# Three of seven half-products of an fp32r feed-forward layer read both parts of their operand in one 512-column pass

## The chip, the cores and the metric

One NeuronCore of one Trainium2 chip runs the whole layer. The metric is device time in microseconds (us) of one execution. Before the change three runs took 820.55, 821.32 and 821.43 us, a median of 821.32 us.

## What is computed

One layer of an encoder on 512 tokens of width 1024, in float32: a half-step SwiGLU feed-forward network (FFN1), a mixer (a Fourier part and attention), a second half-step feed-forward network (FFN2), and a last RMS norm.

```python
def swiglu(h, w_gate, w_up, w_down):
    return (jax.nn.silu(h @ w_gate) * (h @ w_up)) @ w_down

x = x + 0.5 * swiglu(rms_norm(x, ffn1_norm), ffn1_w_gate, ffn1_w_up, ffn1_w_down)
...
x = x + 0.5 * swiglu(rms_norm(x, ffn2_norm), ffn2_w_gate, ffn2_w_up, ffn2_w_down)
```

The hidden width is 2752: 21 blocks of 128 columns and one of 64.

## The kernel before

**Precision.** TensorE multiplies in fp32r, which keeps fewer bits than float32. So each operand is split into a high part (a cast to fp32r) and a low part (the rest), and each product is three matmuls: high weights by high operand, high weights by low operand, low weights by high operand. The high part is cast by ScalarE, the low part subtracted by VectorE (`lows`, L128). Another way to a low part is `rest_by_dma` (L155): ScalarE writes the negated high part, and a DMA from GpSimd's queue adds the weights to it as they come from memory.

**Half-products.** A block j of 128 hidden columns needs a gate product and an up product, each of 128 weights columns by 512 tokens, over 8 chunks of 128 rows. For 35 blocks of the two networks (17 in FFN1, 18 in FFN2) `seven` (L407) makes these two products from seven products of half the tokens (256 columns) and half the rows (4 chunks), with sums and differences of weights' quarters and of the operand's quarters. The weights' names are a11, a12, s1, s2, s4, s3, a22, in order of use; the operand's are b11, b22, b21, t1 to t4, and stand in one tile `rt` with their high and low parts, made once per network in `operands` (L333). `multiply` (L413) makes one half-product: 4 chunks x 3 passes = 12 matmuls of 256 columns, each with a weight load of its own (LDWEIGHTS, "PEld" in the profile). So a block takes 84 matmuls.

**Where the sums are made.** PSUM bank r collects a11, s2, s3 and a22 one after another; ScalarE copies its state out in between (`kept`, L426, and L456, L464). Bank q collects s1 and then s4; bank p2 holds a12. VectorE adds the pieces into the gate `g` (L441, L451) and the up half `u` (L457), multiplies them (L465), and the result is split into `at` (L466, L467). All of these use the first 256 of a bank's 512 columns.

**Order.** PE and SP run in the order of the code, the other engines in an order that the scheduler chose when the kernel was built; each engine takes its instructions strictly in its own order. In `seven`, a block's products run as a11, a12, then a22 of the block before, then s1, s2, s4, s3. Between them `prepare` (L366) makes the next block's weights in eight pieces: raw weights arrive by DMA, VectorE makes the combinations (`combine`, L394), ScalarE casts and VectorE subtracts: three pieces of 1024 columns (`both`, L379: a11 with a12, s1 with s2, s3 with s4) and one of 512 (`single`, L388: a22). a22's weights are needed a whole block later than they are made.

**Stages.** Blocks come in groups. After each group of blocks its down products run (`dn`, L184: 128 weight columns by 512 tokens, three matmuls of 512 columns per chunk). The 512-column passes use `turned` (L177): operand and bank are walked in pieces of 4 columns with a step of 16, four times. Where the 512-column passes read their operand, it starts 4 columns past a multiple of 16 (`NEAR`, `FRONT + LOWER`), and the weights at a multiple of 16; `rt` and its weights both start at a multiple of 16. At the start of each group the second matmul is cut into one of 64 and one of 192 columns (`CUT`, `parts_of`, L160).

## Time and profile before

| | |
|---|---|
| median of three runs | 821.32 us |
| the profiled execution's own time | 820.94 us |
| its span in the profile | 818.9 us |
| PE busy (matmul) | 812.4 us, 99% of the span |
| VectorE busy | 637.5 us, 78% |
| ScalarE busy | 483.1 us, 59% |
| GpSimd busy | 29.3 us, 4% |
| matmuls of the half-products | r 1686, q 840, p 420 pieces |

The profiled execution took 2.0 us more than its span (what lies ahead of the first and behind the last recorded instruction). A row of the groups reads: source line, engine, operation, output tile <- input tiles, shape, count | busy time in us, mean duration of one in ns | idle time before it and what ended that. A matmul's duration is its latency; matmuls are pipelined, so the time from one to the next is shorter, and is read from the chain of work (start, length in us, what, count), where each piece begins as the one ahead of it ends.

### The profile page before, as it was taken

The page shows a single profiled execution, that of the slowest core. Times are in us where ns is not written, and L with a number is a line of the kernel's source. Part 1 is how long each engine was busy: PE and PEld are TensorE (multiplying, and loading weights), DVE is VectorE, ACT ScalarE, POOL GpSimd, SP SyncE. Part 2 cuts the span into 40 slices and gives each one's busy share as a digit, 9 for nine tenths or more (in the row PEclk, how much of TensorE's full clock was granted, in tenths as well). Part 3 has the DMA queues.
Part 4 walks back from the last instruction along what each step waited for, and adds up shares of the span by engine and source line. Part 5 has one row for each costly group of instructions (what it writes and reads, how often), then busy time and mean ns, then how long its engine had stood idle before and what let it go on. Part 6 is the DMA issues. An engine that isn't in the chain of part 4 may idle for free.

```text
span 818.9 us, 13611 instructions
## 1 busy us (share of the span) xinstructions
PE 812.4 (99%) x5362; PEld 746.1 (91%) x5362; DVE 637.5 (78%) x1003; ACT 483.1 (59%) x810; POOL 29.3 (4%) x31
## 2 busy tenths in 40 slices
PE   9999999999999999999999999999999999999997
PEld 7889999899989998889998888899989999899987
DVE  7898896479856847799998578999945896479574
ACT  7763674257523735699998448456632673257462
POOL 0110000000000000221000001100000000000001
PEclk9999999999999999999999999999999999999999
DMA  7664322333141223342101234542232322322222
GB/s 258 174 145 179 124 93 77 124 104 142 59 151 71 90 70 116 129 147 66 65 26 52 77 112 127 123 176 108 94 122 114 127 100 69 132 104 97 69 78 103
DMA packets 31568, 89.97 MB, mean 110 GB/s; under 512 B 3728, under 2 KB 9232, under 8 KB 31504
## 3 DMA queue, kind: packets, MB, share of 16 engines
q1 hardware_dynamic: 27776, 82.61, 29.1%
q0 software_dynamic: 3008, 5.51, 3.7%
q10 hardware_dynamic: 720, 0.98, 0.3%
q8 instruction: 42, 0.69, 0.3%
q14 instruction: 22, 0.18, 0.1%
HBM read 84.24 MB, written 2.10 MB: 105 GB/s over the span
## 4 chain that ended last, share of the span: by engine, by line
PE 95%; DVE 2%; ACT 1%; POOL 1%; issue 1%; DMA 0%; POOLq 0%; DVEq 0%; ACTq 0%
PE dn L184 25%; PE r L420 23%; PE q L420 12%; PE gu L184 8%; PE mix L184 6%; PE p L420 6%; PE gu L709 3%; PE mix L1203 2%; PE mix L1169 2%; PE mix L1007 1%; PE mix L1008 1%; PE mix L1009 1%; PE mix L1066 1%; PE mix L1143 1%; PE mix L1144 1%
## 5 line engine op out<-in xcount | busy, mean ns | idle before, releaser
L420 PE MATMUL r<-rt,ring 128*128 128x256 f32 x1686 | 209.2, 276 | 0.0
L184 PE MATMUL dn<-at,ring 128*128 128x512 f32 x900 | 202.5, 380 | 0.0
L420 PEld LDWEIGHTS r<-rt,ring 128*128 128x128 f32 x1686 | 200.3, 188 | 0.8
L184 PEld LDWEIGHTS dn<-at,ring 128*128 128x128 f32 x900 | 168.0, 188 | 28.3
L420 PE MATMUL q<-rt,ring 128*128 128x256 f32 x840 | 106.6, 276 | 0.0
L128 DVE TENSOR_TENSOR ring<-s,ring 128x1024 fp32r<-128x1024 f32 x70 | 85.5, 1221 | 23.8 <-ACT ring L379 20.8
L420 PEld LDWEIGHTS q<-rt,ring 128*128 128x128 f32 x840 | 100.4, 188 | 0.0
L544 DVE SCALAR_TENSOR_TENSOR gx<-dn,gx 128x512 f32<-128x512 f32 x61 | 41.9, 688 | 67.1 <-PE dn L184 67.1
L379 ACT CAST ring<-s 128x1024 fp32r<-128x1024 f32 x70 | 73.5, 1050 | 28.3 <-PE p L420 13.7
L170 ACT CAST ring<-raw_dn 128x768 fp32r<-128x768 f32 (+3 forms) x58 | 45.3, 784 | 72.8 <-PE dn L184 61.9
L128 DVE TENSOR_TENSOR ring<-raw_dn,ring 128x768 fp32r<-128x768 f32 (+3 forms) x58 | 51.5, 892 | 5.7 <-PE r L420 4.4
L420 PE MATMUL p<-rt,ring 128*128 128x256 f32 x420 | 53.3, 276 | 0.0
L128 DVE TENSOR_TENSOR ring<-raw_g,ring 128x1024 fp32r<-128x1024 f32 x35 | 42.7, 1220 | 11.7 <-PE p L420 10.2
L420 PEld LDWEIGHTS p<-rt,ring 128*128 128x128 f32 x420 | 50.2, 188 | 0.0
L184 PE MATMUL gu<-ring 128*128 128x512 f32 x216 | 48.9, 381 | 0.0
L379 ACT CAST ring<-raw_g 128x1024 fp32r<-128x1024 f32 x35 | 36.8, 1051 | 17.2 <-DMA raw_g<-in_wgu 11.5
L184 PEld LDWEIGHTS gu<-ring 128*128 128x128 f32 x216 | 40.4, 188 | 6.9
L428 ACT COPY p<-r 128x256 f32<-128x256 f32 x35 | 12.9, 369 | 44.9 <-PE r L420 44.6
L452 ACT ACTIVATE g<-g 128x512 f32<-128x512 f32 x35 | 22.2, 633 | 23.9 <-DVE g L451 23.6
L388 ACT CAST ring<-raw_u 128x512 fp32r<-128x512 f32 x35 | 21.8, 624 | 16.0 <-PE q L420 15.7
L184 PE MATMUL mix<-near,ring 128*128 128x512 f32 x120 | 28.8, 381 | 0.0
L465 DVE TENSOR_TENSOR u<-g,u 128x512 f32<-128x512 f32 x35 | 24.0, 687 | 6.1 <-ACT u L464 6.0
(266 smaller groups left out, 1314.3 us busy)
## 6 DMA issues: line engine op xcount, KB each, us to landing
raw_g<-in_wgu SPq DMA_DIRECT2D x35, 512.0 KB, 3.8
raw_u<-in_wgu SPq DMA_DIRECT2D x35, 512.0 KB, 4.3
raw_dn<-in_wd SPq DMA_DIRECT2D x40, 384.0 KB, 3.1
raw_gu<-in_wgu SPq DMA_DIRECT2D x12, 512.0 KB, 3.7
raw_o<-in_wo SPq DMA_DIRECT2D x8, 512.0 KB, 3.5
raw_dn<-in_wd SPq DMA_DIRECT2D x8, 448.0 KB, 3.7
raw_wq<-in_wins SPq DMA_DIRECT2D x4, 512.0 KB, 3.5
raw_f<-in_winf SPq DMA_DIRECT2D x4, 512.0 KB, 3.5
```

Of the source, the lines that this page charges most:

```text
L128: nc.vector.tensor_tensor(out=lo, in0=src, in1=asf(hi), op=ALU.subtract)
L170: nc.scalar.copy(hi[:, :n, :], raw[:, :n, :])
L184: nc.tensor.matmul(ps, a, b, start=first and b is mhi and a is whi, stop=last and a is wlo)
L379: nc.scalar.copy(hi, src)
L388: nc.scalar.copy(hi, src)
L420: nc.tensor.matmul(ps[:, t], a[:, ks], b[:, i, t], start=first and i == 0 and o == 0, stop=i == KH - 1 and o == 2, skip_group_check=not first,
L452: nc.scalar.activation(b["g"], b["g"], AF.Silu)
L465: nc.vector.tensor_tensor(out=u, in0=b["g"], in1=u, op=ALU.mult)
L544: nc.vector.scalar_tensor_tensor(out=x[d][:, t], in0=ps[:, t], scalar=0.5, in1=x[d][:, t], op0=ALU.mult, op1=ALU.add)
L709: nc.tensor.matmul(turned(pss[c]), w[:, k % 2, c], turned(m[k]), start=k == 0 and m is hh and w is hi, stop=k == KD - 1 and w is lo,)
L1169: nc.tensor.transpose(pts[n][:, c * P : (c + 1) * P], prob[t, b, c][:, kc * P : (kc + 1) * P], ident)
L1203: nc.tensor.matmul(turned(outs[t, b]), w, turned(p), start=kc == 0 and i == 0, stop=kc == 3 and i == 1)
```

## The change

Three of the seven, a12, s4 and a22 (`WIDE`), take high weights by both operand parts in one pass: `rt` is laid out so that the high and the low part of a chunk lie side by side (512 columns), and one turned matmul of 512 columns writes high by high into the first half of the bank and high by low into its second half. The low weights by the high part stay a matmul of 256 columns. So these products take 4 x (one of 512 + one of 256) in place of 12 x one of 256. The other four keep their 12 matmuls; only their operand's place changes. What the second half of the bank then holds has to be added: one more VectorE addition of 256 columns for each of the three (`added`, `kept`). And the low part of a22's weights is made by `rest_by_dma` in place of VectorE's subtraction.

```diff
+WIDE = ('a12', 's4', 'a22')
-            rt = ap.tile([P, 7, 2, KH, HALF], F32R, name=f"rt{n_}")
+            rt = ap.tile([P, 7, KH, 2, HALF], F32R, name=f"rt{n_}")
...
-                        h, l = rt[:, c, 0, i], rt[:, c, 1, i]
+                        h, l = rt[:, c, i, 0], rt[:, c, i, 1]
...
                 def single(n, src):
                     t = take()
                     hi, lo = t[:, :S], t[:, S:]
                     nc.scalar.copy(hi, src)
-                    lows(lo, src, hi)
+                    rest_by_dma(lo.rearrange("p (a b) -> p a b", b=P), hi.rearrange("p (a b) -> p a b", b=P), wgu[2 * j + 1][:, KH:])
...
                 def multiply(ps, wn, on, w, first):
-                    (whi, wlo), (mhi, mlo) = w[wn], (part[on][:, i] for i in range(2))
+                    whi, wlo = w[wn]
                     for i in range(KH):
-                        ks = slice(i * P, (i + 1) * P)
-                        for o, (a, b) in enumerate(((whi, mhi), (whi, mlo), (wlo, mhi))):
-                            for t in parts_of(next(count)):
-                                nc.tensor.matmul(
-                                    ps[:, t], a[:, ks], b[:, i, t], start=first and i == 0 and o == 0,
-                                    stop=i == KH - 1 and o == 2, skip_group_check=not first,
-                                )
+                        ks, m = slice(i * P, (i + 1) * P), part[on][:, i].rearrange("p a b -> p (a b)")
+                        start, stop = first and i == 0, i == KH - 1
+                        if wn in WIDE:
+                            nc.tensor.matmul(turned(ps), whi[:, ks], turned(m), start=start, stop=False, skip_group_check=True)
+                        else:
+                            for o in range(2):
+                                for t in parts_of(next(count)):
+                                    nc.tensor.matmul(
+                                        ps[:, t], whi[:, ks], m[:, o * HALF :][:, t], start=start and o == 0, stop=False,
+                                        skip_group_check=True,
+                                    )
+                        nc.tensor.matmul(
+                            ps[:, :HALF], wlo[:, ks], m[:, :HALF], start=False, stop=stop, skip_group_check=True
+                        )
                     give(*w.get((wn, "slots"), ()))

-                def kept(ps, n, j):
-                    t = sp.tile([P, HALF], F32, tag=n, name=f"{n}{n_}_{j}")
-                    nc.scalar.copy(t, ps)
-                    return t
+                def added(out, ps, other, n):
+                    nc.vector.tensor_tensor(out=out, in0=ps[:, :HALF], in1=other, op=ALU.add)
+                    if n in WIDE:
+                        nc.vector.tensor_tensor(out=out, in0=ps[:, HALF:], in1=out, op=ALU.add)
+
+                def kept(out, ps, wide=False):
+                    nc.scalar.copy(out, ps[:, HALF:] if wide else ps[:, :HALF])
+                    if wide:
+                        nc.vector.tensor_tensor(out=out, in0=ps[:, :HALF], in1=out, op=ALU.add)
...
-                        nc.vector.tensor_tensor(out=b["g"][:, HALF:], in0=ps, in1=b["p1"], op=ALU.add)
+                        added(b["g"][:, HALF:], ps, b["p1"], "a12")
...
-                        nc.vector.tensor_tensor(out=b["g"][:, :HALF], in0=b["q"], in1=b["u2"], op=ALU.add)
+                        added(b["g"][:, :HALF], b["q"], b["u2"], "s4")
...
-                        nc.scalar.copy(u[:, HALF:], b["r"])
+                        kept(u[:, HALF:], b["r"], "a22" in WIDE)
```

On PE, at the first products of block 12 of FFN1 (r, p2 and q are the banks, with the block's number behind the first underscore; the last number is a buffer's), there stood before:

```order
L420 MATMUL r0_12_1866<-rt0_129,ring_61 128x256 x12
L420 MATMUL p20_12_1881<-rt0_129,ring_61 128x256 x12
L420 MATMUL r0_11_1744<-rt0_129,ring_61 128x256 x12
L420 MATMUL q0_12_1918<-rt0_129,ring_61 128x256 x12
L420 MATMUL r0_12_1866<-rt0_129,ring_61 128x256 x12
```

Where a11 ends and a12 begins, there stands now:

```order
L425 MATMUL r0_12_1806<-rt0_129,ring_61 128x256 x2
L429 MATMUL r0_12_1806<-rt0_129,ring_61 128x256
L421 MATMUL p20_12_1821<-rt0_129,ring_61 128x4x32x4
L429 MATMUL p20_12_1821<-rt0_129,ring_61 128x256
L421 MATMUL p20_12_1821<-rt0_129,ring_61 128x4x32x4
```

No product moved; in a12, a22 and s4 matmuls of 512 columns (128x4x32x4) and of 256 now alternate, four of each.

On DVE (VectorE), from the gate's sum of block 12 on, there stood before:

```order
L441 TENSOR_TENSOR g0_12_1894<-p20_12_1881,p10_12_1879 128x256
L128 TENSOR_TENSOR ring_61<-raw_g0_13_1860,ring_61 128x1024
L465 TENSOR_TENSOR u0_11_1855<-g0_11_1772,u0_11_1855 128x512
L128 TENSOR_TENSOR ring_61<-s12_0_13_1864,ring_61 128x1024
L128 TENSOR_TENSOR ring_61<-raw_u0_13_1861,ring_61 128x512
L128 TENSOR_TENSOR at0_128<-u0_11_1855,at0_128 128x512
L394 TENSOR_TENSOR s12_0_14_1986<-raw_u0_14_1983 128x512
L451 TENSOR_TENSOR g0_12_1894<-q0_12_1918,u20_12_1945 128x256
L128 TENSOR_TENSOR ring_61<-s34_0_13_1865,ring_61 128x1024
```

There stands now:

```order
L435 TENSOR_TENSOR g0_12_1830<-p20_12_1821,p10_12_1807 128x256
L129 TENSOR_TENSOR ring_61<-raw_g0_13_1800,ring_61 128x1024
L437 TENSOR_TENSOR g0_12_1830<-p20_12_1821,g0_12_1830 128x256
L442 TENSOR_TENSOR u0_11_1795<-r0_11_1692,u0_11_1795 128x256
L129 TENSOR_TENSOR ring_61<-s12_0_13_1804,ring_61 128x1024
L486 TENSOR_TENSOR u0_11_1795<-g0_11_1716,u0_11_1795 128x512
L395 TENSOR_TENSOR s12_0_14_1918<-raw_u0_14_1915 128x512
L435 TENSOR_TENSOR g0_12_1830<-q0_12_1852,u20_12_1879 128x256
L395 TENSOR_TENSOR s12_0_14_1918<-s12_0_14_1918,raw_g0_14_1914 128x512
L437 TENSOR_TENSOR g0_12_1830<-q0_12_1852,g0_12_1830 128x256
L129 TENSOR_TENSOR at0_128<-u0_11_1795,at0_128 128x512
L129 TENSOR_TENSOR ring_61<-s34_0_13_1805,ring_61 128x1024
```

The three additions (L437 twice, L442) are new, the low part of a22's weights (`ring<-raw_u`) is gone, and the low part of s3 and s4 (`ring<-s34`) stands a few rows later.

On ACT (ScalarE), around the copies of bank q (p5) and of bank r (u2) in block 12, there stood before:

```order
L388 CAST ring_61<-raw_u0_13_1861 128x512
L428 COPY p50_12_1931<-q0_12_1918 128x256
L466 CAST at0_128<-u0_11_1855 128x512
L428 COPY u20_12_1945<-r0_12_1866 128x256
L379 CAST ring_61<-s34_0_13_1865 128x1024
```

There stands now:

```order
L389 CAST ring_61<-raw_u0_13_1801 128x512
L440 COPY p50_12_1853<-q0_12_1852 128x256
L158 ACTIVATE ring_61<-ring_61 128x512
L440 COPY u20_12_1879<-r0_12_1806 128x256
L380 CAST ring_61<-s34_0_13_1805 128x1024
L487 CAST at0_128<-u0_11_1795 128x512
```

The negated copy (L158) has come ahead of the copy of r, and the cast of `at` has gone behind the cast of s34.

More of the change, by code (lines that the diff above doesn't have):

```diff
@@ L431, in step, with part_tile @@
+                def kept(out, ps, wide=False):
+                    nc.scalar.copy(out, ps[:, HALF:] if wide else ps[:, :HALF])
+                    if wide:
+                        nc.vector.tensor_tensor(out=out, in0=ps[:, :HALF], in1=out, op=ALU.add)
+                def part_tile(n, j):
+                    return sp.tile([P, HALF], F32, tag=n, name=f"{n}{n_}_{j}")
                 def step(j, w, n):
@@ L433, in step @@
                     if n == 0:
-                        b["r"] = bank(f"r{n_}_{j}")[:, :HALF]
+                        b["r"], b["p1"] = bank(f"r{n_}_{j}"), part_tile("p1", j)
                         multiply(b["r"], "a11", "b11", w, True)
-                        b["p1"] = kept(b["r"], "p1", j)
+                        kept(b["p1"], b["r"])
                     elif n == 1:
-                        ps = bank(f"p2{n_}_{j}")[:, :HALF]
+                        ps = bank(f"p2{n_}_{j}")
                         multiply(ps, "a12", "b21", w, True)
                         b["g"] = tp.tile([P, S], F32, tag="g", name=f"g{n_}_{j}")
-                        nc.vector.tensor_tensor(out=b["g"][:, HALF:], in0=ps, in1=b["p1"], op=ALU.add)
+                        added(b["g"][:, HALF:], ps, b["p1"], "a12")
                     elif n == 3:
-                        b["q"] = bank(f"q{n_}_{j}")[:, :HALF]
+                        b["q"], b["p5"] = bank(f"q{n_}_{j}"), part_tile("p5", j)
                         multiply(b["q"], "s1", "t1", w, True)
-                        b["p5"] = kept(b["q"], "p5", j)
+                        kept(b["p5"], b["q"])
                     elif n == 4:
                         multiply(b["r"], "s2", "t2", w, False)
-                        b["u2"] = kept(b["r"], "u2", j)
+                        b["u2"] = part_tile("u2", j)
+                        kept(b["u2"], b["r"])
                     elif n == 5:
                         multiply(b["q"], "s4", "b22", w, False)
-                        nc.vector.tensor_tensor(out=b["g"][:, :HALF], in0=b["q"], in1=b["u2"], op=ALU.add)
+                        added(b["g"][:, :HALF], b["q"], b["u2"], "s4")
                         nc.scalar.activation(b["g"], b["g"], AF.Silu)
@@ L455, in step @@
                         b["u"] = tp.tile([P, S], F32, tag="u", name=f"u{n_}_{j}")
-                        nc.scalar.copy(b["u"][:, :HALF], b["r"])
-                        nc.vector.tensor_tensor(
-                            out=b["u"][:, :HALF], in0=b["u"][:, :HALF], in1=b["p5"], op=ALU.add
-                        )
+                        u = b["u"][:, :HALF]
+                        if "s3" in WIDE:
+                            nc.scalar.copy(b["u"], b["r"])
+                            nc.vector.tensor_tensor(out=u, in0=u, in1=b["u"][:, HALF:], op=ALU.add)
+                            nc.vector.tensor_tensor(out=u, in0=u, in1=b["p5"], op=ALU.add)
+                        else:
+                            nc.scalar.copy(u, b["r"][:, :HALF])
+                            nc.vector.tensor_tensor(out=u, in0=u, in1=b["p5"], op=ALU.add)
                     elif n == 9:
```

## The prediction, made before the result was known

> **What bounds the kernel now.** I read the page first, for the engines' shares, then who waited for whom, then the chain of work, for the pace. Two lines of the page:
>
> ```profile
> span 818.9 us, 13611 instructions
> PE 812.4 (99%) x5362; PEld 746.1 (91%) x5362; DVE 637.5 (78%) x1003; ACT 483.1 (59%) x810; POOL 29.3 (4%) x31
> ```
>
> and all rows in which PE waited for anything:
>
> ```profile
> PE busy L654 <- PEq L1519: 0.8, 1, 0.8
> PE mix L1143 <- DVE near L128: 0.2, 1, 0.2
> ```
>
> TensorE is never waited into idleness in the half-products. Its busy share alone would not say that it is at its pace, but the two waits of 1.0 us in all do. So the time is the sum of the start-to-start times of the matmuls, and the chain gives these:
>
> ```profile
> 75.65 1.36 PE p L420 x12
> 130.05 3.96 PE dn L184 x18
> 134.01 1.37 PE r L420 x12
> 135.38 27.72 PE dn L184 x126
> ```
>
> In a long run a pass of 256 columns takes 1.36 us / 12 = 113.3 ns and one of 512 columns 3.96 us / 18 = 220.0 ns. From 256 to 512 columns 106.7 ns are added, so a pass has 113.3 - 106.7 = 6.7 ns on top of its columns. That is all that the change can save on TensorE.
>
> The skill says otherwise about this size: the Trainium skill, "TensorE: Matmul & The Clock Gate", section "Back-to-back issue gap", puts the fixed part of a pass at 2.5 ns. By that the joined passes would save 420 x 2.5 = 1.05 us in place of the 2.8 us below. The rows above measure 6.7 ns in this kernel's fp32r stream, and the measurement decides.
>
> **Part 1, the joined passes.** 35 blocks x 3 products x 4 chunks = 420 times, three passes of 256 (340.0 ns) become one of 512 and one of 256: 220.0 + 113.3 = 333.3 ns. If both kept the pace of their long runs, that would be 420 x 6.7 = 2.8 us less. But nowhere in the half-products of before do single passes of 512 and 256 alternate, so the pace of the mix is the unknown price, and I bound it by the nearest rows: the first passes behind a change of length, and stretches in which lengths change often. The groups of instructions, asked for narrow stretches of time, give mean durations. First the moment at 135.2 us where 512 follows 256, then the one at 133.86 us where 256 follows 512:
>
> ```profile
> L184 PE MATMUL dn<-at,ring 128*128 128x512 f32 x1 | 0.4, 384 | 0.0
> L420 PE MATMUL r<-rt,ring 128*128 128x256 f32 x1 | 0.3, 279 | 0.0
> L184 PE MATMUL dn<-at,ring 128*128 128x512 f32 x900 | 202.5, 380 | 0.0
> L420 PE MATMUL p<-rt,ring 128*128 128x256 f32 x420 | 53.3, 276 | 0.0
> ```
>
> The first pass of 512 takes 384 ns against 380 in the long run, the first of 256 takes 279 against 276: some 3 ns each. The chain agrees: the twelve of r between two runs of dn stand with 1.37 us, the twelve of p inside a run of 256 with 1.36. If each change of length costs this, and in an alternation every pass is a first one, a pair takes 333.3 + 4 + 3 = 340 ns, as much as the three passes had: no change.
>
> Above that bound stand the stretches where lengths change often, from 415 to 420 us in the mixer, and one long stretch of 512 (340.3 to 343.4 us) that runs at another pace than its neighbour (345.2 to 350.2 us):
>
> ```profile
> L1066 PE MATMUL mix<-pos,near 128*128 128x256 f32 x8 | 1.3, 281 | 0.0
> L1066 PE MATMUL mix<-both,near 128*128 128x512 f32 x4 | 1.2, 386 | 0.0
> ...
> L184 PE MATMUL mix<-ring 128*128 128x512 f32 x15 | 3.7, 393 | 0.0
> ...
> L184 PE MATMUL mix<-ring,more 128*128 128x512 f32 x21 | 4.9, 380 | 0.0
> ```
>
> In the mixed stretch 256 columns take 281 (5 over) and 512 take 386 (6 over): a pair of 333.3 + 11 = 344.3 ns, 4.3 more than before, 420 x 4.3 = 1.8 us slower. The same instruction at 393 and at 380 ns, with nothing waited for, says that the pass of 512 has two paces 13 ns apart, and stays in the one that it fell into. If all wide passes fell into the slow one, a pair would take 333.3 + 13 + 3 = 349 ns, 420 x 9.3 = 3.9 us slower. I read this as the moving operand and the next weights, which load during the pass, getting into each other's way at some offsets. In the code the 512-column passes read an operand that starts 4 columns past a multiple of 16, while `rt` and its weights both start on one; the changed kernel's wide passes have no such offset.
>
> Of the ends, -6.7, 0, +4.3 and +9.3 ns a pair, I take the mixed stretch, +4.3, because it is the only row whose lengths change as often as in the new products: **+1.8 us**.
>
> The wide pass also writes its bank in pieces of four columns (`turned`). A rule speaks against that: the Trainium skill, "SBUF — State Buffer", section "Door 1: The DMA port swizzle", says that any non-contiguous access pattern of PSUM slows matmuls significantly. By it the wide passes would be slower than 220 ns for this reason too; the 900 turned passes of dn, at 220.0 ns, do not show it, so I add nothing, and give it 1 chance in 100 inside the slow rival.
>
> **Part 2, VectorE.** It gains three additions of 256 columns for each block and loses one subtraction of 512. Its own times from start to start, in a stretch without idle time:
>
> ```profile
> 193.71 1.22 DVE L128 TENSOR_TENSOR ring<-raw_g,ring 128x1024 fp32r<-128x1024 f32 x1
> 194.84 0.42 DVE L441 TENSOR_TENSOR g<-p,p 128x256 f32<-128x256 f32 x1
> 195.18 0.95 DVE L128 TENSOR_TENSOR ring<-raw_dn,ring 128x768 fp32r<-128x768 f32 x1
> 196.04 1.22 DVE L128 TENSOR_TENSOR ring<-s,ring 128x1024 fp32r<-128x1024 f32 x1
> 197.18 0.69 DVE L465 TENSOR_TENSOR u<-g,u 128x512 f32<-128x512 f32 x1
> 197.78 0.68 DVE L128 TENSOR_TENSOR ring<-raw_u,ring 128x512 fp32r<-128x512 f32 x1
> 198.38 0.68 DVE L394 TENSOR_TENSOR s<-raw_u 128x512 f32<-128x512 f32 x1
> ```
>
> So 1024 columns take 1.13 us, 512 take 0.60 and 256 take 0.34. A block has 3 of 1024, 7 of 512 and 3 of 256: 3.39 + 4.20 + 1.02 = 8.61 us. After it has 3, 6 and 6: 9.03 us. A block of products takes 84 x 113.3 ns = 9.52 us on TensorE, and with the pair above 48 x 113.3 + 12 x 344.3 ns = 9.57 us. VectorE stays below it, at 94%. The windows of the first group show the room, block by block:
>
> ```profile
> core 0: us, PE busy (x) PEld busy (x) DVE busy (x) ACT busy (x) POOL busy (x), PEclk, DMA share, GB/s
> 112.37:121.89 9.52, 9.52 (x86) 9.52 (x86) 9.52 (x14) 8.29 (x14) 0.00 (x0) 1.00 0.37 124
> sum 55.89, PE 55.89 PEld 55.89 DVE 49.85 ACT 35.55 POOL 0.00; mean PE 9.31 PEld 9.31 DVE 8.31 ACT 5.93 POOL 0.00
> ```
>
> VectorE was busy for 49.85 of 55.89 us. It gets 6 blocks x 1.02 - 5 x 0.60 = 3.1 us more: 53.0. One window was full already, and TensorE did not wait in it, because weights are ready early. Cost: 0, covered by that lead. If the lead were used up, the price is at most the excess of a block, 0.42 us x 35 = 14.7 us.
>
> **Part 3, ScalarE, GpSimd and the transfer.** The negated copy of 512 columns takes ScalarE 0.54 us a block (186.27 to 186.81 below); a block's share in the windows is 5.93 of 9.31 us, so there is room. Its place matters more: it waits for s2's weights to be read and stands ahead of the copy of r (u2), for which s3 waits.
>
> ```profile
> 186.27 0.63 ACT L388 CAST ring<-raw_u 128x512 fp32r<-128x512 f32 x1
> 186.81 0.36 ACT L428 COPY p<-q 128x256 f32<-128x256 f32 x1
> 187.06 0.62 ACT L466 CAST at<-u 128x512 fp32r<-128x512 f32 x1
> 187.75 0.37 ACT L428 COPY u<-r 128x256 f32<-128x256 f32 x1
> ...
> 186.35 1.36 PE r L420 x12
> 187.71 1.36 PE q L420 x12
> 189.07 2.72 PE r L420 x24
> ```
>
> u2's copy ended at 188.12, s3 begins in the chain at 189.07: 0.95 us to spare. Put behind the negated copy it ends some 0.45 us later; 0.5 us stays, and s4, between them, gets no shorter. What is queued behind (s34's cast, the cast of `at`) has microseconds of lead. Cost 0; without the cover up to 0.45 us a block. The DMA:
>
> ```profile
> L158 POOL DMA_DIRECT2D ring<-in_wgu x3: 863/889/927, 35.9 to 500.6; - x3
> ring<-in_wgu POOLq DMA_DIRECT2D x3, 512.0 KB, 5.3
> 212.19 1.36 PE r L420 x12
> DMA packets 31568, 89.97 MB, mean 110 GB/s; under 512 B 3728, under 2 KB 9232, under 8 KB 31504
> ```
>
> GpSimd takes 0.9 us to issue one, and 512 KB landed 5.3 us later; ours is 256 KB. The subtraction that it replaces ended at 198.46 us, and these weights' product began at 212.19: 13.7 us of lead against some 7. GpSimd has nothing else queued there. Cost 0. It adds 35 x 256 KB = 9 MB to the 90 MB moved, at a DMA share of 0.37 in the densest of those windows.
>
> At the end of FFN2 the last block's result is needed 10 passes and more after its product; one addition (0.34 us) is put into that chain: 0 to 0.3 us, once, counted as 0.
>
> **Sum.** 820.94 us (the profiled execution; the median is 0.4 us above it) + 1.8 = **822.7 us**.
>
> **The rivals.**
> 1. *The mix keeps the pace of the long runs* (faster). For it: the 113.3 and 220.0 ns stood over thousands of passes. Against it: each change of length in the half-products cost 3 to 4 ns. It gives 820.94 - 2.8 = 818.1 us. It decides below 333.3 + 2.8 = 336.1 ns a pair, where the gain passes 0.2%. Chance 0.30.
> 2. *The change of length costs exactly what it saves* (340 ns): 820.9 us, nothing seen. Chance 0.18, with the clean transitions for it.
> 3. *VectorE becomes the bound.* At 94% and with the lead in weights, little speaks for it: some 0.2 us a block would give 828. Chance 0.04.
> 4. *The slow pace of 512* (349 ns), perhaps with a few slow passes of 256 behind each wide product: 820.94 + 3.9 = 824.8, up to 827. It is the upper half of the forecast's own case.
>
> **How the numbers follow.** The forecast, a pair between 340 and 349 ns, has 0.48, of which 0.08 falls within 0.2%. About 0.2% (1.6 us) is what a measurement of this kernel can tell from no change. Faster: rival 1 less the 0.02 of it that ends too small, 0.28. Same: 0.18 + 0.08 + 0.02 = 0.28. Slower: 0.40 + 0.04 = 0.44. The likeliest case alone spans 821 to 825.5 us; the range takes in rival 1 at its full size and the lower part of what lies beyond rival 4: 818.1 to 826.0.
>
> **What would show it.** In the profile after, the groups of L421 (512) and L429 (256) give the pair: durations near 386 and 281 for the forecast, 380 and 276 for rival 1, 384 and 279 for rival 2, 393 for rival 4. The chain gives a wide product with 1.38 us against 1.33, 1.36 and 1.40. PE's list of waits should stay empty in the half-products; a row with DVE or ACT there of over a microsecond would be rival 3, or the u2 copy, and would make parts 2 and 3 wrong. A wait of L421 for a DMA would make the 7 us of the transfer wrong. The passes of 256 in the four unchanged products should stay at 276 ns; more would mean that the wide passes spoil their neighbours, which I have not counted.

## The result, and the profile after

| | before | after |
|---|---|---|
| median | 821.24 us (4 runs) | 826.55 us (4 runs: 825.27, 825.61, 827.49, 827.53) |
| the profiled execution's own time | 820.94 us | 825.27 us |
| its span | 818.9 us | 823.5 us |

The ratio is 1.0062, with a 95% interval from 1.0047 to 1.0077: slower by 5.3 us. The prediction was 822.7 us, with a range up to 826.0: the sign was its likeliest one, the size was outside. The profiled execution is the fastest of the four, 1.3 us below the median, so it accounts for 4.3 of the 5.3 us (4.6 by the spans); what the slower ones have on top no trace shows.

The same views as before, first the page: shares of the engines, and all rows in which PE waited.

```profile
span 823.5 us, 12954 instructions
PE 815.7 (99%) x4942; PEld 733.7 (89%) x4942; DVE 654.0 (79%) x1073; ACT 500.6 (61%) x845; POOL 59.5 (7%) x66
```

```profile
PE busy L675 <- PEq L1540: 0.8, 1, 0.8
PE gu L730 <- ACT ring L716: 0.7, 1, 0.7
PE dn L185 <- DVE ring L129: 0.7, 2, 0.5
```

No wait stands in the half-products (r, q, p), as before; there TensorE is slower without waiting. Two rows are new: one wait ahead of a gate or up product that is not made of halves (gu), and two waits in the down stages (dn). The loss in the half-products must be pace, and the chain shows it. Here are the first pieces of the seven products of a period and of the a12 behind them (start, length, what; a piece is one wide pass, or the first two of a product's narrow ones):

```profile
173.88 0.22 PE p L421
...
175.26 0.22 PE r L421
...
176.65 0.24 PE q L425 x2
...
178.03 0.23 PE r L425 x2
...
179.38 0.23 PE q L421
...
180.77 0.24 PE r L425 x2
...
182.15 0.23 PE r L425 x2
...
183.50 0.23 PE p L421
```

From start to start the joined products (a12 at 173.88, a22 of the block before at 175.26, s4 at 179.38) take 1.38, 1.39 and 1.39 us, 4.16 in all, where three products of twelve narrow passes took 4.08. The products behind them take 1.38 (s1, at 176.65) and 1.38 (s3, at 180.77), though nothing in them changed but their operand's place; s2 and a11, which stand behind a narrow product, take 1.35 each, the old pace. The period is 9.62 us, where the prediction's 84 passes of 113.3 ns make 9.52. 35 blocks by 0.10 us are 3.5 us. The whole sum agrees: the distances from each matmul's start to the next one's, added up over all half-products of the trace, are 334.0 us before and 337.75 after.

The groups give the durations of the passes:

```profile
L421 PE MATMUL p<-rt,ring 128*128 128x512 f32 x140 | 49.8, 385 | 0.0
L429 PE MATMUL p<-rt,ring 128*128 128x256 f32 x140 | 39.7, 283 | 0.0
L425 PE MATMUL r<-rt,ring 128*128 128x256 f32 x834 | 146.8, 277 | 0.0
L425 PE MATMUL q<-rt,ring 128*128 128x256 f32 x280 | 49.9, 278 | 0.0
```

The wide pass has 385 ns (380 in a long run), the narrow one between two wide ones 283 (276): 5 and 7 over. A pair is 333.3 + 12 = 345 by the durations, and 4.16 us / 12 = 346.7 ns by the chain. The unchanged products (L425) have 277 and 278, not 276.

The other piece of the loss is in the down stages, at two places. The larger one, 0.79 us by the starts, is in the down stage behind the first group of half-products. The chain around the stall:

```profile
143.99 3.31 PE dn L185 x15
...
148.19 0.97 DVE ring L129
...
149.18 4.97 DMA raw_u<-in_wgu
...
154.78 0.68 DVE s L395
155.47 0.88 DVE ring L129
...
156.39 3.80 PE dn L185 x16
```

TensorE waits for a low part of the down weights (`ring` by L129). VectorE makes it at 155.47, in its order, behind the combinations of the next block's weights (`s`), and these wait for a load of raw weights that was issued at 149.18 and took 4.97 us. Before, the two loads of this kind in the stretch from 146 to 157 us were issued and landed so:

```profile
L371 SPq DMA_DIRECT2D raw_u<-in_wgu x2: 328/328/328, 148.9 to 154.7; - x2
...
DMA to landing us min/median/max: 3.4/3.5/3.6
```

The same load was issued 0.3 us earlier, at 148.9, and took at most 3.6 us. VectorE's low part that frees its buffer began earlier by as much (147.94 against 148.19), so in the change the load was not late in its stage: it was long. In the lists of waits it has the first of these rows before and the second one after:

```profile
DVE s L394 <- DMA raw_u<-in_wgu: 2.1, 4, 0.6
```

```profile
DVE s L395 <- DMA raw_u<-in_wgu: 4.8, 6, 2.0
```

VectorE waited for it 2.0 us at the longest, against 0.6. The list of DMA queues shows what else was fetched then, from 149 to 155 us in both, after and before:

```profile
q8 instruction: 1, 0.02, 1.8%
```

```profile
q14 instruction: 1, 0.01, 0.3%
```

In the change a fetch of 16 KB of instructions on queue q8 begins at 150.09 us, inside the load, and takes 1.77 us; before, this queue's fetches begin at 134.72 and 161.55 us, outside it. Between two fetches of q8 TensorE gets through some 255 instructions, so they are taken for TensorE's own code; the change has 840 instructions less there (420 matmuls and their weight loads), and the fetches fall elsewhere. Fourteen kernels were profiled for this document. In the eight that have a q8 fetch inside this load it takes 4.6 to 5.1 us, in the other six 3.5 to 3.7. None of the added VectorE instructions stands in this stretch. How a fetch lengthens a load is not shown, and not every one does: before, one that began at 612.9 us, 0.2 us ahead of a load, left it at 3.5 us.

The smaller place, 0.56 us, is the first down stage of FFN2. There VectorE works without a pause from 529.8 to 539.9 us, and a low part of the down weights for which TensorE waits stands behind one of 1024 columns for the next block:

```profile
535.64 1.22 DVE L129 TENSOR_TENSOR ring<-s,ring 128x1024 fp32r<-128x1024 f32 x1
536.77 0.42 DVE L129 TENSOR_TENSOR ring<-raw_dn,ring 128x256 fp32r<-128x256 f32 x1
```

No block of half-products of FFN2 has run by then, so here too none of the three additions is in VectorE's way; its order is another than before, and how the change brought that about stays open.

The down stages take 216.64 us from start to start, 1.37 more than the 215.27 of before. So the account of the profiled execution is: half-products +3.75, down stages +1.37, the gate and up products that are not made of halves (gu) -0.6 (85.2 against 85.8), all else near 0. The sum is 4.5 us, and the spans differ by 4.6.

### The profile page after: what moved, and what is told of

Its sections match the earlier page's. It is cut to its first block, busy times and chain, and to the rows that moved or that the text cites. A ratio compares the mean times of both kernels' runs of the same rounds, so it can differ in the third digit from the quotient of the medians.

```text
span 823.5 us, 12954 instructions
## 1 busy us (share of the span) xinstructions
PE 815.7 (99%) x4942; PEld 733.7 (89%) x4942; DVE 654.0 (79%) x1073; ACT 500.6 (61%) x845; POOL 59.5 (7%) x66
## 4 chain that ended last, share of the span: by engine, by line
PE 88%; DVE 6%; ACT 2%; DMA 2%; issue 1%; POOL 1%; POOLq 0%; DVEq 0%; ACTq 0%; SPq 0%
PE dn L185 23%; PE r L425 12%; PE r L429 8%; PE mix L185 6%; PE q L429 4%; PE q L425 4%; PE gu L185 4%; PE r L421 4%; PE p L421 4%; PE q L421 4%; PE gu L730 3%; PE p L429 2%; PE mix L1224 2%; PE mix L1190 2%; DVE ring L129 1%
## 5 line engine op out<-in xcount | busy, mean ns | idle before, releaser
L429 PE MATMUL r<-rt,ring 128*128 128x256 f32 x560 | 156.0, 279 | 0.0
L425 PE MATMUL r<-rt,ring 128*128 128x256 f32 x846 | 147.9, 276 | 0.0
L425 PEld LDWEIGHTS r<-rt,ring 128*128 128x128 f32 x846 | 128.2, 188 | 1.7
L429 PEld LDWEIGHTS r<-rt,ring 128*128 128x128 f32 x560 | 105.2, 188 | 0.2
L129 DVE TENSOR_TENSOR ring<-s,ring 128x1024 fp32r<-128x1024 f32 x70 | 85.5, 1222 | 14.1 <-ACT ring L380 11.8
L429 PE MATMUL q<-rt,ring 128*128 128x256 f32 x280 | 78.4, 280 | 0.0
L159 POOL DMA_DIRECT2D ring<-in_wgu x38 | 32.8, 864 | 479.3 <-ACT u L440 426.8
L129 DVE TENSOR_TENSOR ring<-raw_dn,ring 128x768 fp32r<-128x768 f32 (+3 forms) x58 | 51.6, 893 | 9.0 <-ACT ring L171 4.5
L429 PEld LDWEIGHTS q<-rt,ring 128*128 128x128 f32 x280 | 52.6, 188 | 0.0
L129 DVE TENSOR_TENSOR ring<-raw_g,ring 128x1024 fp32r<-128x1024 f32 x35 | 42.8, 1223 | 12.1 <-PE p L421 10.3
L421 PE MATMUL r<-rt,ring 128*128 128x512 f32 x140 | 49.9, 385 | 0.0
L425 PE MATMUL q<-rt,ring 128*128 128x256 f32 x280 | 49.9, 278 | 0.0
L421 PE MATMUL p<-rt,ring 128*128 128x512 f32 x140 | 49.8, 385 | 0.0
L421 PE MATMUL q<-rt,ring 128*128 128x512 f32 x140 | 49.8, 385 | 0.0
```

What stands on the lines that cost most here:

```text
L129: nc.vector.tensor_tensor(out=lo, in0=src, in1=asf(hi), op=ALU.subtract)
L159: nc.gpsimd.dma_start(out=lo, in_=src, accum_op=ALU.add)
L421: nc.tensor.matmul(turned(ps), whi[:, ks], turned(m), start=start, stop=False, skip_group_check=True)
L425: nc.tensor.matmul(ps[:, t], whi[:, ks], m[:, o * HALF :][:, t], start=start and o == 0, stop=False, skip_group_check=True,)
L429: nc.tensor.matmul(ps[:, :HALF], wlo[:, ks], m[:, :HALF], start=False, stop=stop, skip_group_check=True)
```

## The experiments

Three things were to be told apart. For the pace of the joined products: **theory A**, the moving operand and the weights loaded during the pass are in each other's way, depending on where they stand (the prediction's reading), against **theory B**, each change of length costs a sum of its own. For the down stages: VectorE's added work against the other edits. For the transfer: whether its copy costs anything in ScalarE's queue. All sums of starts below are made as above; the edits are against the changed kernel unless it is said otherwise.

**All of `rt` moved by 4 columns**, so that every operand of the half-products has the offset that the other passes of 512 have.

```diff
-            rt = ap.tile([P, 7, KH, 2, HALF], F32R, name=f"rt{n_}")
+            rtw = ap.tile([P, 7 * KH * 2 * HALF + 16], F32R, name=f"rt{n_}")
+            rt = rtw[:, NEAR : NEAR + 7 * KH * 2 * HALF].rearrange("p (n k a b) -> p n k a b", k=KH, a=2, b=HALF)
```

> The changed kernel, with the operand tile rt moved by 4 columns (16 bytes), so that it no longer starts at the same offset as the weights, as the operands of the other 512-column passes do; nothing else differs. Theory A, the operand and the weights that load beside it clash at equal offsets: the wide passes come near 220 ns and the passes of 256 behind them near 113 to 116, seven's stages lose 3 us or more, 822 us or less. Theory B, every change of length costs, wherever the operand lies: pairs stay at some 346 ns and the time at 826.5 us. Theory C, a late weight or transfer in the down stages makes the loss: the 1.4 us there stay under either.

Measured: 832.80 us, ratio 1.0137 (1.0118 to 1.0157). Two groups, an unchanged product and a wide pass:

```profile
L426 PE MATMUL r<-rt,ring 128*128 128x256 f32 x834 | 152.9, 282 | 0.0
L422 PE MATMUL p<-rt,ring 128*128 128x512 f32 x140 | 49.4, 386 | 0.0
```

The offset matters a great deal, and it is the wrong way round: the narrow passes of the unchanged products go from 277 to 282 ns, and the wide ones are no faster. In the form in which the prediction had it ("the changed kernel's wide passes have no such offset") theory A is wrong.

**Lengths grouped:** four wide passes and then four narrow ones, two changes of length a product in place of eight.

```diff
                             nc.tensor.matmul(turned(ps), whi[:, ks], turned(m), start=start, stop=False, skip_group_check=True)
+                            continue
...
+                    for i in range(KH if wn in WIDE else 0):
+                        nc.tensor.matmul(
+                            ps[:, :HALF], wlo[:, i * P : (i + 1) * P], part[on][:, i, 0], start=False, stop=i == KH - 1, skip_group_check=True
+                        )
```

> The changed kernel, but a wide product makes its four passes of 512 first and then its four of 256: the same work with 2 changes of length in place of 8. Theory B (each change of length costs 4 to 9 ns): three of four pairs lose their extra 13 ns, 315 x 13 = 4 us less, some 822.5 us. Theory A (offsets, whatever the order): the passes of 512 stay at 224 or rise to 233, the passes of 256 at 122, no gain of over 1 us.

Measured: 826.56 us, ratio 1.0059 (1.0044 to 1.0074), as slow as the change itself.

```profile
L421 PE MATMUL p<-rt,ring 128*128 128x512 f32 x140 | 37.3, 387 | 0.0
L426 PE MATMUL r<-rt,ring 128*128 128x256 f32 x834 | 148.7, 278 | 0.0
```

The wide passes stand side by side here and have 387 ns, more than in the alternation. The half-products take 339.0 us. Theory B falls: a quarter of the changes of length, and nothing gained.

**a22's low part by VectorE again**, the joined passes kept.

```diff
-                    rest_by_dma(lo.rearrange("p (a b) -> p a b", b=P), hi.rearrange("p (a b) -> p a b", b=P), wgu[2 * j + 1][:, KH:])
+                    lows(lo, src, hi)
```

> The changed kernel with a22's low part by VectorE again, no accumulating transfer: undoes one part alone. Theory C (the transfer or the order that it brings makes the stalls in the down stages): the waits of dn for VectorE go, 1 to 1.4 us less, 825.3 us; VectorE would be at 9.6 us a block against 9.65 on TensorE, so that if VectorE's load were the cause, new waits of TensorE appear in the half-products and the time rises by 2 us or more. Theories A and B: seven's pace is unchanged to 0.3 us.

Measured: 828.05 us, ratio 1.0079 (1.0061 to 1.0096). The half-products are unmoved (337.9 us); the down stages go to 218.5, and PE waits for VectorE there:

```profile
PE dn L185 <- DVE ring L129: 1.2, 2, 0.7
PE dn L185 <- DVE at L129: 0.2, 1, 0.2
```

So without the transfer the down stages cost 1.8 us more. It is a help, not a burden.

**No product joined**, layout and transfer kept.

```diff
-WIDE = ('a12', 's4', 'a22')
+WIDE = ()
```

> The changed kernel with no product joined: the new layout of rt and the accumulating transfer alone, 12 passes of 256 in every product. All theories of the joined passes (A and B): seven runs at 113.4 ns a pass again, the time is that of before plus what the transfer costs in the down stages, 821.2 to 822.5 us. If the layout of rt itself slows the passes, they stand above 114 ns and the time above 823 us.

Measured: 827.45 us, ratio 1.0065 (1.0048 to 1.0082). That was a surprise: not one joined pass, and as slow as the change. The waits of PE in the half-products, and then one group of passes twice, from 263.5 to 274 us and from 282.4 to 293 us, ahead of one of these waits (near 275 us) and behind it:

```profile
PE r L425 <- ACT u L440: 1.9, 4, 1.1
PE r L425 <- ACT u L479: 0.6, 1, 0.6
```

```profile
L425 PE MATMUL q<-rt,ring 128*128 128x256 f32 x16 | 2.8, 276 | 0.0
```

```profile
L425 PE MATMUL q<-rt,ring 128*128 128x256 f32 x16 | 2.9, 281 | 0.0
```

TensorE waits five times for a copy by ScalarE, 2.5 us in all. And the same group of passes on the same operand has 276 ns ahead of the wait and 281 behind it: 113.3 and 117.8 ns from start to start, up to the end of the group of blocks at 302 us. So a run of narrow passes has two paces, and can keep the one that it falls into. Which one follows a wait is not settled by the wait's length: behind the longest, 1.1 us near 199 us, the same group has 276 ns again (200 to 211 us), while a delay of 0.16 us at 577 us left the passes at 117.8 ns until 597 us. The half-products take 341.0 us, 7.0 more than before. By the starts, the delayed passes and the ones right behind them make 5.2 us of this, and the two slow stretches 1.8.

**The layout alone:** no product joined, a22's low part by VectorE (both edits above).

> The changed kernel with no product joined and a22's low part by VectorE: of the change only the layout of rt is left. In the run with the transfer and no joined pass, TensorE waited for ScalarE's copies 2.5 us and stayed at 117 to 118 ns a pass in the blocks behind each wait. Theory D (the negated copy in ScalarE's queue is what delays those copies): here the waits are gone, every block at 113.3 ns, the time that of before, 820.9 to 821.6 us. If the layout of rt is at fault, blocks stand above 114 ns and the time stays above 825.

Measured: 821.31 us, ratio 1.0006 (0.9994 to 1.0018), with no wait for ScalarE in the half-products and this group:

```profile
L425 PE MATMUL q<-rt,ring 128*128 128x256 f32 x560 | 98.9, 276 | 0.0
```

The layout costs nothing. The loss of the run before belongs to the transfer in the absence of the joined passes: its negated copy is one instruction more in ScalarE's order, ahead of the copies that release r. At the longest wait a cast of down weights, which had itself waited 1.38 us for a load, stands ahead of both. Whether the copy's length or the order that the scheduler chose around it does the damage was not tried.

**The three joined operands moved off their multiple of 16 columns:** b22 and b21 by 4, t4 by 20. To make room t1, t2 and t3, operands of unchanged products, move by 16; b11, the operand of a11, keeps its place.

```diff
+            rts = (0, 1, entries(0, 1, 0)), (1, 3, entries(1, 3, 4)), (3, 6, entries(3, 6, 16)), (6, 7, entries(6, 7, 16 + 4))
...
-            part = {n: rt[:, i] for i, n in enumerate(("b11", "b22", "b21", "t1", "t2", "t3", "t4"))}
+            part = {n: next(r[:, i - a] for a, z, r in rts if a <= i < z) for i, n in enumerate(("b11", "b22", "b21", "t1", "t2", "t3", "t4"))}
```

> The changed kernel, with only the three operand quarters of the joined products (b22, b21, t4) moved by 4 columns, those of the other four left where they were. Moving all of rt slowed the passes of the four unjoined products to 119 ns and left the joined ones at 227. Theory A in its narrower form (a wide pass wants the offset, a pass of 256 does not): pairs at 333 to 340 ns, unjoined passes at 113.3, 822 us or less. Theory B (alternating lengths cost, wherever the operand lies): pairs stay near 345 ns, 825 to 828 us.

Measured: 831.99 us, ratio 1.0138 (1.0117 to 1.0158). A joined product's wide pass, and an unchanged product:

```profile
L427 PE MATMUL p<-rt,ring 128*128 128x512 f32 x140 | 49.6, 386 | 0.0
L431 PE MATMUL q<-rt,ring 128*128 128x256 f32 x280 | 51.8, 282 | 0.0
```

The pairs take 343.6 ns by the starts, so theory A falls in its narrower form too. And the unchanged products have 282 ns, 118.6 from start to start. They are not all alike. s1, s2 and s3, whose operands moved by 16 columns, take 1.43 to 1.44 us each and settle nowhere. a11, whose operand did not move, is back at 113.3 ns from its fifth pass on and takes 1.38, though it stands right behind s3. So here the slow pace goes with the operand's place rather than with the passes ahead, and a shift by 16 columns is enough to change it.

**Plain order:** the wide pass without `turned`, reading 512 columns in a row and writing the bank in a row.

```diff
-                            nc.tensor.matmul(turned(ps), whi[:, ks], turned(m), start=start, stop=False, skip_group_check=True)
+                            nc.tensor.matmul(ps, whi[:, ks], m, start=start, stop=False, skip_group_check=True)
```

> The changed kernel with the joined passes' 512 columns in plain order in place of the turned one. If the order of columns matters to the clash between operand and weights, the passes of 512 move from 224 to the 233 ns that plain passes of 512 had in the mixer, 420 x 9 = 4 us slower, 830 us; if the loss is by the change of length alone, the pair stays at 346 ns and the time at 826.5 us.

Measured: 834.37 us, ratio 1.0158 (1.0138 to 1.0179).

```profile
L421 PE MATMUL p<-rt,ring 128*128 128x512 f32 x140 | 51.0, 397 | 0.0
```

397 ns against the turned pass's 385, at the same place and with the same weights: the order in which operand and bank are walked makes 12 ns. The rule that the prediction had weighed, the Trainium skill, "SBUF — State Buffer", section "Door 1: The DMA port swizzle" (a non-contiguous pattern in PSUM slows matmuls), would have it the other way round; here the contiguous pass is the slower one, with the operand's order changed along with the bank's.

**No change of length inside a joined product:** the low weights too run over 512 columns.

```diff
+                        if wn in WIDE:
+                            nc.tensor.matmul(turned(ps), wlo[:, ks], turned(m), start=False, stop=stop, skip_group_check=True)
+                            continue
```

> The changed kernel, but the low weights too read both parts in one pass of 512 (it adds the product of the two low parts): a joined product is eight passes of 512, with no change of length inside. It adds 420 x 107 = 45 us of columns. Theory B: passes of 512 at 220.0 ns but for the first of a product, pairs at 440 ns, 826.5 + 420 x (440 - 346) = 866 us. Theory A (equal offsets clash): 224 to 234 ns a pass also here, 867 to 877 us.

Measured: 870.97 us, ratio 1.0604 (1.0583 to 1.0625).

```profile
L421 PE MATMUL p<-rt,ring 128*128 128x512 f32 x140 | 54.4, 389 | 0.0
L430 PE MATMUL p<-rt,ring 128*128 128x512 f32 x140 | 54.2, 388 | 0.0
L430 PE MATMUL r<-rt,ring 128*128 128x512 f32 x140 | 54.1, 386 | 0.0
```

Passes of 512 in a run of eight do not have the 380 ns of the down stages but 386 to 389; from start to start 227.2 ns on the mean, in a pattern that repeats every eight passes (in block 12: 228, 233, 229, 220, 224, 227, 233, 230). The loss of the wide pass needs no change of length.

**The same with the operands moved** as above: those of a12 and s4 by 4 columns, that of a22 by 20.

> The joined products run all their passes over 512 columns (the low weights times both parts, so the product of the two low parts is added), as in the kernel whose passes of 512 took 227.1 ns on the mean, and the operands of these three products lie 4 columns further on, as in the kernel that was 10.8 us slower than before by that shift alone. If the offset between operand and weights sets the pace, the passes of 512 leave the mean of 227: to 220 (time 866) if the offset that the other products of passes of 512 have in this kernel is the right one, or to 230 and more (time 873 and over) if it is the wrong one. If the offset matters only where passes of both lengths meet, the passes stay at 227 and the time at 871 within 1 us.

Measured: 875.52 us, ratio 1.0661 (1.0647 to 1.0675). The wide passes of a12 (p, high and low weights) and, as the worst, of a22 (r, low weights):

```profile
L427 PE MATMUL p<-rt,ring 128*128 128x512 f32 x140 | 53.3, 381 | 0.0
L436 PE MATMUL p<-rt,ring 128*128 128x512 f32 x140 | 53.2, 380 | 0.0
L436 PE MATMUL r<-rt,ring 128*128 128x512 f32 x140 | 55.3, 395 | 0.0
```

Neither side of the expectation holds as a whole. For a12 it does: four columns take its passes from 389 and 388 to 381 and 380, the 220 ns of a long run. s4, with the same four columns, stays at 389 and 388, and a22's low weights go from 386 to 395. So the place of the operand matters, but does not decide alone; the place of the weights or of the bank, or what the passes ahead left, must come into it. The unchanged products are at 118 ns from start to start, and the whole is slower.

**One product joined**, a12, with a22's low part by VectorE.

```diff
-WIDE = ('a12', 's4', 'a22')
+WIDE = ('a12',)
...
-                    rest_by_dma(lo.rearrange("p (a b) -> p a b", b=P), hi.rearrange("p (a b) -> p a b", b=P), wgu[2 * j + 1][:, KH:])
+                    lows(lo, src, hi)
```

> One product of a block, the one with a12, keeps the joined passes (140 of the 420 pairs); s4 and a22 go back to passes of 256, and a22's low part is VectorE's again. If each joined product brings its own loss, in its pairs and in the run of passes behind it, and the products do not act on each other, a third of the loss in the half-products stays: 3.75 us / 3 = 1.25 us over the 334.0 us of before, and VectorE has one addition more a block where the change had three: about 1 us in the down stages if its additions cost there (three cost 3.2 us). Sum some 2.2 us, a ratio of 1.0015 to 1.004. If a run of passes of 256 keeps a slow pace until something disturbs it, a single joined product can also leave whole blocks at 117 to 118 ns (each block up to 0.35 us, 35 blocks up to 12 us): a ratio of 1.005 to 1.015. If the loss came from having three of them, the ratio is 1.000.

Measured: 822.31 us, ratio 1.0013 (1.0003 to 1.0023).

```profile
L421 PE MATMUL p<-rt,ring 128*128 128x512 f32 x140 | 49.7, 385 | 0.0
```

The half-products take 335.4 us, 1.4 more than before, a third of the change's 3.75 (1.25) within 0.2. Each joined product brings its own loss. One addition in place of three leaves the down stages at 215.4: no loss there.

**The kernel before without its one divided pass**, to see whether a change of length is enough to start the slow pace.

```diff
-CUT = 1, P // 2
+CUT = -1, P // 2
```

> The kernel before, without its one divided pass (64 and 192 columns in place of 256) at the head of each group of blocks; no joined product is in it. If a run of passes of 256 has two paces and keeps the one that it falls into, some groups should now run at 117 to 118 ns a pass instead of 113.3: each group of 500 passes that does so costs 500 x 4.5 ns = 2.2 us, six groups at most 13 us, and the kernel is slower by 2 to 13 us. If a slow pace comes only from the mixture of lengths, the runs settle in a few passes and the time stays within 0.3 us of before.

Measured: 820.78 us, ratio 1.0001 (0.9992 to 1.0011). The half-products take 333.2 us, at 113.3 ns throughout. A group that starts behind the down stages' 512 columns falls into the fast pace by itself, with and without the divided pass; the 0.8 us saved come back as waits elsewhere:

```profile
PE gu L709 <- ACT ring L695: 1.3, 1, 1.3
PE dn L184 <- DVE ring L128: 0.5, 1, 0.5
```

The second of these waits, in a down stage of FFN2, has the same chain as the stall of the changed kernel:

```profile
612.60 4.96 DMA raw_u<-in_wgu
...
618.87 0.88 DVE ring L128
```

A fetch on q8 begins at 612.57 us, within 0.03 us of the load. So six matmuls less are enough to bring this stall about, with no joined pass, no transfer and no addition in the kernel.

**The kernel before with three additions more on VectorE** for each block, repetitions of ones that are there.

```diff
                         nc.vector.tensor_tensor(out=b["g"][:, HALF:], in0=ps, in1=b["p1"], op=ALU.add)
+                        nc.vector.tensor_tensor(out=b["g"][:, HALF:], in0=ps, in1=b["p1"], op=ALU.add)
...
                         nc.vector.tensor_tensor(out=b["g"][:, :HALF], in0=b["q"], in1=b["u2"], op=ALU.add)
+                        nc.vector.tensor_tensor(out=b["g"][:, :HALF], in0=b["q"], in1=b["u2"], op=ALU.add)
+                        nc.vector.tensor_tensor(out=b["g"][:, :HALF], in0=b["q"], in1=b["u2"], op=ALU.add)
```

> The kernel before, with three additions of 256 columns more a block on VectorE, each a repetition of one that is there (the results do not change); no joined pass, no transfer, the old layout. It measures VectorE's load alone. If the loss in the down stages comes from VectorE's additions, the half-products stay at 334.0 us and the down stages go from 215.3 us to 217 to 218.5 (as where the change was made without the transfer: 218.5): 823 to 824.5 us. If VectorE's lead covers them, as the prediction put it, the time stays at 821.3 within 0.5 us, and the down stages' loss belongs to the joined passes or to the transfers.

Measured: 825.05 us, ratio 1.0055 (1.0038 to 1.0073). The half-products stay at 334.6 us; the down stages go to 218.7, 3.5 us more, of which 2.1 are this wait:

```profile
PE dn L184 <- DVE at L128: 2.1, 3, 0.8
```

Three additions of 256 columns a block cost 3.5 us in the down stages, with no joined pass and no transfer: VectorE comes out of a group of blocks late (in the first group it leads the chain from 127.35 to 134.31 us), and TensorE waits for the last block's result (`at`). VectorE's lead does not cover these 1.02 us a block. The load that was long in the change takes 3.7 us here, and the stall behind it is not there.

No version beat both kernels: the layout alone and the kernel before without its divided pass are as fast as before, all others slower.

## Why the prediction was wrong

The steps that failed are three terms of the sum. The pairs, +1.8 us, measured 2.65. The passes behind the joined products stood at nothing, with no reason given, and measured 1.1. The stages outside the half-products stood at nothing, and the down stages measured 1.4 (`gu` took 0.6 less).

**The fixed part, 6.7 ns a pass: a right reading, of no use.** The passes that would show it, 113.3 and 220.0 ns, never came in the alternation. So this figure was not to be had. The 2.5 ns that the prediction quotes from the Trainium skill, "TensorE: Matmul & The Clock Gate", section "Back-to-back issue gap", stand there for a single isolated matmul, not for a stream, and no run here shows them.

**"I take the mixed stretch, +4.3".** The nearest row, and the right sign, but too small: the pair has 346.7 ns, +6.7, between the mixed stretch and the slow pace (+9.3). 420 pairs by 6.7 ns are 2.8 us in place of 1.8. By the starts it is 225.1 and 121.2, 346.3 ns or 2.65 us, so the two readings agree within 0.15 us. The durations were foretold as 386 and 281 and are 385 and 283. The mechanism given for it was half right. That the place of the operand changes the pace is shown (4 columns took the wide passes of a12 from 389 to 381 ns, 20 columns those of a22's low weights from 386 to 395). That the lack of a 4-column offset was the fault is wrong (with it the kernel lost 6 us more). That it is the weights' load that the operand meets was only argued; no run took the load away.

**"More would mean that the wide passes spoil their neighbours, which I have not counted".** They do, and this term of the sum was missing: the narrow products behind a joined one take 1.38 us in place of 1.36, twice a block. By the starts, the 1586 passes of 256 that have a pass of 256 on both sides have 114.1 ns, 0.7 over: 1.1 us. With the 2.65 of the pairs that is the 3.75 of the half-products.

**"Cost: 0, covered by that lead".** For the change this held as far as its trace shows: no product waits for VectorE's sums, and no added instruction stands between VectorE's last pause and either stall of the down stages. But the lead has a limit that the windows over the blocks of the first group do not show, since they end ahead of the down stages: the change adds 0.42 us a block by the prediction's rows, and the 1.02 us of three additions by themselves cost 3.5 us there. What the sum left out are the down stages: 1.4 us as changed. 0.79 of it is a load of 4.97 us, which goes with an instruction fetch that the change has moved; 0.56 is VectorE's new order ahead of FFN2, of open origin.

**Transfer and negated copy: 0, "covered".** Right for the change, in which TensorE waits for neither; without the transfer the down stages took 1.8 us more. But the cover was thin: without the joined passes the same edit brought 2.5 us of waits for ScalarE, and the slow pace behind one of them.

**The sum.** 820.94 + 2.65 (pairs) + 1.1 (neighbours) + 1.4 (down stages) - 0.6 (gu) = 825.5 us; the profiled execution took 825.27. Against the prediction's 1.8 the pairs cost 0.85 us more, and 2.5 us lay in two terms that stood at 0.

**What stays open.** Which property of the places of operand, weights and bank puts a pass on 220, 227 or 235 ns; why a narrow run settles to 113.3 ns within some four passes in the change, and stays near 118 with operands shifted by 4 or by 16 columns; which delay leaves a run in the slow pace; how an instruction fetch lengthens a load; and the 2 us between the executions of the changed kernel.

## What to carry to other kernels

Joining passes to save a fixed part of some 7 ns only pays if the new pass keeps its pace beside its new neighbours; price it from a stretch of such neighbours, and price the passes behind it as well. A lead covers added work only up to a size: here 0.42 us a block raised no wait for its results, and 1.02 us a block did, at the first instruction of the next stage that stands behind it. An edit that takes instructions away also moves the instruction fetches, so a stall that appears after it need not come from the work that it added: look at the load behind the stall, and at a run with that work alone. And an edit that costs nothing in company may cost its full price alone, so undo parts one by one before the loss is put down to the one that looks heaviest.

## What the hardware showed beside this

The same product with the same operand ran at 113.3 or at 117.8 ns a pass for whole blocks. In the kernel with no joined product one delay left 276 ns ahead of it and 281 behind it, and the longest delay left no trace in the pace. The delays cost more than the waits in the list: 5.2 us by the starts, where the list has 2.5. A load of 512 KB took 4.6 to 5.1 us in the eight kernels with a 16 KB instruction fetch inside it, and 3.5 to 3.7 in the six without. A pass of 512 columns came out at 380, 385, 389, 395 and 397 ns with nothing waited for, by the place of its operand, the order of its columns and the passes beside it.
